# Token forms of the second half in two pieces, with weight forms between them, and another order of the first block's products

## The chip, the cores and the metric

One Trainium2 chip, of which the kernel uses one core. The metric is device microseconds from launch to end of one execution, lower is better. The core has a matrix engine (TensorE, PE in the profile; its weight loads are PEld), VectorE (DVE), ScalarE (ACT), GpSimd (POOL) and SyncE (SP); each works through its own instruction queue in order and waits on semaphores of the others. POOL and SP issue the transfers between the chip's main memory and the on-chip buffers.

## What is computed

Two pre-norm residual layers on 1024 tokens of width 1024, and a final norm, all in float32. The parts that the change touches are the channel MLP of both layers and the input projection of the second layer's gating unit:

```python
for layer in range(DEPTH):                      # DEPTH = 2
    h = rms_norm(x, mix_norm[layer])
    if layer % 2 == 0:
        ...                                     # gated recurrence and attention
    else:
        gated = chunked_gmlp(h @ gm_w_in[o], gm_ln_g[o], gm_ln_b[o], gm_ws[o], gm_bs[o])
        mix = gated @ gm_w_out[o]
    x = x + mix
    h = rms_norm(x, mlp_norm[layer])
    x = x + jnp.square(jax.nn.relu(h @ mlp_w1[layer])) @ mlp_w2[layer]
return rms_norm(x, final_norm)
```

`chunked_gmlp` applies gelu to both halves of its input, a layer norm to the second (`v`), mixes `v` inside chunks of 128 tokens and multiplies.

## The kernel before

**Tokens and halves.** The activations stand with features on partitions, in two token halves of 512: half 0 and half 1, each as four tiles of 128 x 1024 (`xp[half]`, two feature blocks of 512 columns in one tile).

**Split numbers.** Every matmul operand is split into a high part (rounded by ScalarE to the fp32r type) and a low part (VectorE: value minus high part). A product of two split operands takes three matmuls (`mm3`: L181 high x high, L182, L183 with the low parts). A *form* is such a pair of tiles: token forms (`make_form`, L190 and L191) and weight forms (`split2`, L738 and L739; high part `whi` on ScalarE, low part `wlo` on VectorE).

**Seven products.** Big products are done by a seven-product scheme of Strassen's kind on 2 x 2 blocks, named P1 to P7. Each of the seven needs a token form (two tiles, `k2` = 0 and 1: a sum or difference of half 0 and half 1) and a weight form (a sum of weight quarters). P1 and P2 need half 0 only. P7 needs the difference inside half 1, and P6, P5, P4 and P3 are made from it on VectorE one after another, by sums and splits (`half1_forms`).

**Stages.** `inward` computes the MLP's first product in column blocks b = 0, 1, ... of 512 hidden features; (b,p) is product p of block b, 24 matmuls. `gmlp` does the gating unit's `v` projection, with weights moving and tokens stationary; there a product comes in two steps kp = 0, 1, (p,kp), 24 matmuls each. `outward` brings the MLP back to 1024 features and prepares half 0 of the next stage while it ends, so that P1 and P2 can start at once.

**The entries.** Half 1 of a stage's input is complete only as the stage begins. Its norm and token forms are therefore made by a `lead`, a list of three steps that `inward` and `gmlp` run ahead of their first three products: sums of squares, `rms1` (the norm's factor) and `forms1`. `forms1` spreads the factor over a tile (`spread`, L767), scales half 1 with eight VectorE instructions (`scaled`, L772) and makes all of P7, P6, P5, P4 and P3 (`half1_forms`, L845 to L866). This happens at three places: entry I (first layer's MLP, from about 611 us), entry II (`gmlp`, about 1290) and entry III (second layer's MLP, about 2070). The second call of `inward` (the gating unit's `u` half) has no lead.

**What sets the order.** The program text is written in the order in which work is wanted, and the framework then puts each engine's queue in order by its own estimate of when things are ready, so neighbouring products' matmuls can stand interleaved. Ahead of each product the weight forms of the next two are asked for (`LEAD = 2`); ahead of a lead step, those of the product itself and one more. A group's weights come from `a_forms` in the fixed order P1, P2, P7, P6, P4, P5, P3, since each sum builds on the one before (L888, L891, L894, L896). There are three buffers for weight forms (`U_W`), six for raw weights (`U_RAW`), four accumulators of two PSUM banks (`pair_ps`) that also serve the norm. Results of the first products are held back (`held`) until the third product is issued, and then taken out by `after1` (`evict` in `gmlp`): a copy by ScalarE (L944, L1220) or an addition by VectorE (L1006, L1225), a further VectorE step for relu squared (L1007), and a store by POOL (L939).

The order of the first two blocks before is (0,P1), (0,P2), (1,P1), (1,P2), (0,P6), (0,P7), (0,P5), (0,P4), (0,P3), (1,P6), (1,P7), (1,P5), (1,P4), (1,P3).

Of the kernel before, what the change touches and what calls it, by code (L numbers as in the profile page):

```python
# [109 lines left out]
def trunk(tc, x_in, mix_norm, mlp_norm, w1, w2, ab_in, ab_out, lb_logits, hgrn_norm,  # L110
# [4 lines left out]
    with ctx:  # L115
# [575 lines left out]
        P1, P2, P6, P7, P5, P4, P3 = range(7)  # L691
        SEQ = [P1, P2, P6, P7, P5, P4, P3]
# [100 lines left out]
        def make_form(f, k2, src):  # L793
            t = new_form(f, k2)
            split(t.hi, t.lo, src)

        class Entry:
# [31 lines left out]
                self.r = self.rms(1, one_bank)  # L829

            def forms1(self):
                half1_forms(self.gcol, spread(self.r, self.two[1][1], one_bank()))

                spare.extend(self.two[1][::-1])

            def lead(self):
                return [lambda: self.squares(1, (0, 1)), self.rms1, self.forms1]

        spare = []

        def half1_forms(gcol, rb):
            for m2 in range(4):
                spill(1, m2)
            for k2 in range(2):
                for k0 in (0, 2):  # L845
                    for j in range(2):
                        scaled(1, 2 * (k0 + k2) + j, gcol, rb)

            sums = [u_tile("fh") for k2 in range(2)]
            b11, b21, b12, b22 = xp[0][0:2], xp[0][2:4], xp[1][0:2], xp[1][2:4]  # L850
            for k2 in range(2):
                vec.tensor_tensor(out=sums[k2], in0=b22[k2], in1=b12[k2], op=ALU.subtract)
                make_form(P7, k2, sums[k2])
            make_form(P3, 0, b22[0])
            for k2 in range(2):
                vec.scalar_tensor_tensor(out=sums[k2], in0=sums[k2], scalar=-1.0, in1=b11[k2],
                                         op0=ALU.mult, op1=ALU.subtract)
                make_form(P6, k2, sums[k2])
            for k2 in range(2):
                vec.tensor_tensor(out=b12[k2], in0=b11[k2], in1=b12[k2], op=ALU.subtract)  # L860
                make_form(P5, k2, b12[k2])
            for k2 in range(2):
                vec.scalar_tensor_tensor(out=sums[k2], in0=sums[k2], scalar=-1.0, in1=b21[k2],
                                         op0=ALU.mult, op1=ALU.subtract)
                make_form(P4, k2, sums[k2])
            make_form(P3, 1, b22[1])  # L866

        def one_bank():
            return pair_ps()[:, 0, :]
# [33 lines left out]
        def inward(ww, NB, finish, lead, last, extra={}):  # L903
# [66 lines left out]
                                             op0=ALU.mult, op1=ALU.subtract)  # L970
                    store(P4, b, t4)

            order = []
            for b in range(NB):
                todo = [(b, p) for p in SEQ if b != 1 or p not in (P1, P2) or not lead]
                if b == 0 and lead:
                    todo[2:2] = [(1, P1), (1, P2)]
                order += todo
            LEAD = 2
            held = []  # L980
            for i, (b, p) in enumerate(order):
                if i < len(lead):
                    for b2, p2_ in order[i:i + LEAD]:
                        form1(b2, p2_)
                    lead[i]()
                for b2, p2_ in order[i:i + 1 + LEAD]:
                    form1(b2, p2_)
                finish(b, None, None, p, order[i + 1:i + 3], None)
                if i == len(order) - 1:
                    last()  # L990
                held.append((b, p, product1(b, p)))
                if i >= len(lead) - 1:
                    while held:
                        after1(*held.pop(0))
                if p == P6 and b in extra:
                    extra[b]()
# [165 lines left out]
        def gmlp(lead):  # L1162
# [69 lines left out]
            tiles, acc, held = {}, {}, []  # L1232
            for n, (u, p, kp) in enumerate(order):
                if n < len(lead):
                    for o in order[n:n + 2]:
                        form_v(*o)
                    lead[n]()
                for o in order[n:n + 3]:
                    form_v(*o)
                a = form_v(u, p, kp)  # L1240
                fresh = p in (P1, P7, P2)
                if fresh and kp == 0:
                    acc[u, p] = [pair_ps() for _ in range(2)]
                elif kp == 0:
                    acc[u, p] = acc[u, {P6: P1, P5: P6, P3: P5, P4: P7}[p]]
                f = form[p, kp]
                for c in range(2):
                    ps = acc[u, p][c]
                    for s in range(2):
                        tok = slice((2 * c + s) * P, (2 * c + s + 1) * P)  # L1250
                        for k in range(2):
                            mm3(ps[:, s, :], (f.hi[:, k, tok], f.lo[:, k, tok]),
                                (a.hi[:, k, :], a.lo[:, k, :]),
                                fresh and kp == k == 0, kp == k == 1, not fresh)
                if kp == 1:
                    held.append((u, p))
                if n >= len(lead) - 1:
                    while held:
                        evict(*held.pop(0))
            for tb in range(8):  # L1260
# [163 lines left out]
```

## Time and profile before

| | us |
|---|---|
| median of 3 runs | 2743.43 |
| the three runs | 2742.97, 2743.43, 2746.48 |
| the profiled execution | 2744.25 |
| its span, first to last instruction | 2742.3 |
| TensorE busy in the span | 2640.1 |
| VectorE busy | 1820.9 |
| ScalarE busy | 1019.4 |

The profile is one execution on the core. Its timeline view lists instructions of one engine in order of time, with the idle time before them and what ended it in brackets; the view of waits adds these up by who waited for whom; the view of stretches gives each engine's busy time and TensorE's granted clock (1.00 is 2.4 GHz, 0.50 is 1.2 GHz) in chosen stretches. Matmuls overlap: one starts every 0.23 us or so and is shown as 0.39 long.

### The profile page before, as it was taken

How to read it: one execution, taken by the hardware profiler on the slowest of the kernel's cores; microseconds unless marked ns; L12 is line 12 of the kernel's file. 1: busy time of each engine (PE TensorE's matmuls, PEld its weight loads, DVE VectorE, ACT ScalarE, POOL GpSimd, SP SyncE). 2: the span in 40 equal slices, each digit the busy share in tenths (PEclk: the TensorE clock that was granted, in tenths of full speed). 3: DMA queues.
4: the chain of work that ended last, by engine and by line, in shares of the span. 5: the costliest groups of instructions: out<-in, count | busy, mean ns of one | idle time of the engine just before them, and what ended most of it. 6: DMA issues, size and time to landing. Idle time of an engine off the chain costs nothing.

```text
span 2742.3 us, 31530 instructions
## 1 busy us (share of the span) xinstructions
PE 2640.1 (96%) x12489; PEld 2143.1 (78%) x12489; DVE 1820.9 (66%) x2046; ACT 1019.4 (37%) x1281; POOL 152.5 (6%) x261
## 2 busy tenths in 40 slices
PE   8999999997999999999899999999997999999998
PEld 7888867685888878887688887877876888878887
DVE  4545464756766687777855666677778666687774
ACT  4212144543333343343433454443334333343343
POOL 1000000000101100000000100000000111000000
PEclk9999999998999999999999999999998999999999
DMA  4111111332545383444233454565431544483341
GB/s 153 43 32 47 43 35 58 108 108 68 184 140 183 124 301 131 159 162 145 73 119 114 138 194 161 191 255 199 169 131 59 167 151 141 160 305 117 131 159 62
DMA packets 204826, 371.62 MB, mean 136 GB/s; under 512 B 12072, under 2 KB 120328, under 8 KB 204680
## 3 DMA queue, kind: packets, MB, share of 16 engines
q1 hardware_dynamic: 173896, 257.93, 28.5%
q0 software_dynamic: 30784, 111.69, 10.5%
q8 instruction: 98, 1.61, 0.2%
q14 instruction: 48, 0.39, 0.0%
HBM read 253.71 MB, written 115.87 MB: 135 GB/s over the span
## 4 chain that ended last, share of the span: by engine, by line
PE 83%; DVE 9%; issue 3%; DMA 3%; ACT 2%; POOL 0%; SPq 0%; DVEq 0%; ACTq 0%; POOLq 0%
PE acc L182 21%; PE acc L183 21%; PE acc L181 21%; PE mm L181 4%; PE mm L183 4%; PE mm L182 4%; PE sm L393 1%; DVE e L551 1%; PE acc L1354 1%; DVE sig L555 1%; DVE x L772 1%; DMA nx<-v_d 1%; PE po L181 1%; DMA fr<-in_gm_w_out 1%; ACT whi L738 0%
## 5 line engine op out<-in xcount | busy, mean ns | idle before, releaser
L738 ACT ACTIVATE whi<-raw 128x1024 fp32r<-128x1024 f32 x273 | 288.6, 1058 | 956.9 <-PE acc L182 754.0
L739 DVE TENSOR_TENSOR wlo<-raw,whi 128x1024 fp32r<-128x1024 f32 x273 | 333.3, 1221 | 392.8 <-ACT whi L738 389.4
L181 PE MATMUL acc<-f1h,whi 128*128 128x512 f32 x1144 | 454.6, 398 | 11.9 <-ACT f1h L738 8.0
L182 PE MATMUL acc<-f1l,whi 128*128 128x512 f32 x1144 | 454.5, 397 | 2.0 <-DVE f1l L739 1.8
L183 PE MATMUL acc<-f1h,wlo 128*128 128x512 f32 x1144 | 453.7, 397 | 0.4 <-DVE wlo L739 0.4
L181 PEld LDWEIGHTS acc<-f1h,whi 128*128 128x128 f32 x1144 | 214.9, 188 | 67.0 <-ACT f1h L738 10.6
L182 PEld LDWEIGHTS acc<-f1l,whi 128*128 128x128 f32 x1144 | 215.3, 188 | 57.2 <-DVE f1l L739 4.0
L183 PEld LDWEIGHTS acc<-f1h,wlo 128*128 128x128 f32 x1144 | 215.3, 188 | 53.8 <-DVE wlo L739 1.1
L182 PE MATMUL acc<-f1l,fh 128*128 128x512 f32 x616 | 243.7, 396 | 0.0
L181 PE MATMUL acc<-f1h,fh 128*128 128x512 f32 x616 | 243.5, 395 | 0.0
L183 PE MATMUL acc<-f1h,fl 128*128 128x512 f32 x616 | 243.4, 395 | 0.0
L1065 DVE TENSOR_TENSOR x<-x,acc 128x1024 f32<-128x1024 f32 x154 | 187.1, 1215 | 34.9 <-PE acc L183 27.0
L181 PE MATMUL mm<-ah,whi 128*128 128x512 f32 x448 | 181.6, 405 | 0.0
L739 DVE TENSOR_TENSOR f1l<-fb,f1h 128x1024 fp32r<-128x1024 f32 x154 | 181.2, 1217 | 0.2 <-ACT f1h L738 0.2
L183 PE MATMUL mm<-ah,wlo 128*128 128x512 f32 x448 | 179.5, 401 | 0.0
L182 PE MATMUL mm<-al,whi 128*128 128x512 f32 x448 | 178.7, 399 | 0.0
L738 ACT ACTIVATE f1h<-fb 128x1024 fp32r<-128x1024 f32 x154 | 152.0, 1044 | 12.2 <-DMA fb<-f_d 12.2
L181 PEld LDWEIGHTS acc<-f1h,fh 128*128 128x128 f32 x616 | 116.0, 188 | 28.5
L182 PEld LDWEIGHTS acc<-f1l,fh 128*128 128x128 f32 x616 | 115.7, 188 | 28.5
L183 PEld LDWEIGHTS acc<-f1h,fl 128*128 128x128 f32 x616 | 115.7, 188 | 28.2
L939 POOL DMA_DIRECT2D f_d<-x x150 | 80.1, 534 | 751.6 <-DVE x L1007 351.9
L65 DVE TENSOR_TENSOR wlo<-raw,whi 128x1024 fp32r<-128x1024 f32 x44 | 53.8, 1222 | 100.8 <-ACT whi L64 80.7
(281 smaller groups left out, 4903.3 us busy)
## 6 DMA issues: line engine op xcount, KB each, us to landing
fb<-f_d SPq DMA_DIRECT2D x154, 512.0 KB, 4.8
f_d<-x POOLq DMA_DIRECT2D x150, 512.0 KB, 3.3
raw<-in_mlp_w SPq DMA_DIRECT2D x96, 512.0 KB, 4.6
raw<-in_gm_w_in SPq DMA_DIRECT2D x54, 512.0 KB, 4.6
fr<-in_mlp_w SPq DMA_DIRECT2D x32, 512.0 KB, 10.1
raw<-in_ab_w_in SPq DMA_DIRECT2D x28, 512.0 KB, 4.4
x_d<-x POOLq DMA_DIRECT2D x24, 512.0 KB, 2.9
x<-x_d SPq DMA_DIRECT2D x24, 512.0 KB, 7.4
```

The source lines that it names most:

```text
L65: nc.vector.tensor_tensor(out=lo, in0=raw, in1=hi.bitcast(F32), op=ALU.subtract)
L181: pe.matmul(out=ps, lhsT=a[0], rhs=b[0], start=start, stop=False, skip_group_check=s)
L182: pe.matmul(out=ps, lhsT=a[0], rhs=b[1], start=False, stop=False, skip_group_check=s)
L183: last_mm[0] = pe.matmul(out=ps, lhsT=a[1], rhs=b[0], start=False, stop=stop, skip_group_check=s)
L393: mm = pe.matmul(out=p3[:, c, :].rearrange("p (b m) -> p b m", m=m), lhsT=kr[:, c * P:(c + 1) * P], rhs=qv[:, c, :, 1, :], start=True, sto ...
L551: vec.tensor_tensor_scan(out=e[:, 0:w][:, ::-1], data0=keep[:, 0:w][:, ::-1], data1=d1[:, ::-1], initial=init, op0=ALU.mult, op1=ALU.max)
L555: vec.tensor_tensor(out=sig[:, 0:w], in0=sig[:, 0:w], in1=e[:, 1:w + 1], op=ALU.mult)
L738: in_turn("hi", lambda: act.activation(t.hi, raw, AF.Copy))
L739: vec.tensor_tensor(out=t.lo, in0=raw, in1=t.hi.bitcast(F32), op=ALU.subtract)
L772: vec.scalar_tensor_tensor(out=xt[half][k], in0=xt[half][k], scalar=gn[:, gcol + k:gcol + k + 1], in1=rb, op0=ALU.mult, op1=ALU.mult)
L939: nc.gpsimd.dma_start(out=f_d[f][b], in_=flat(t))
L1065: last_add[0] = vec.tensor_tensor(out=t, in0=t, in1=ps, op=op)
```

## The change

`half1_forms` becomes a generator that stops once, after the P7 forms; the rest (P3's first form, P6, P5, P4, P3's second) becomes a fourth lead step, `forms2`. The weight forms asked for ahead of the third and fourth lead step reach one product further (`(i > 1)`, and the same in `gmlp`). With a lead, the first two blocks of `inward` take another order: (1,P2) moves behind (0,P6), P7 comes before P6, and both stand right behind (1,P1). Results are still held until the third product. In `gmlp` the order of products stays.

```diff
@@ -829,12 +829,16 @@
                 self.r = self.rms(1, one_bank)
 
             def forms1(self):
-                half1_forms(self.gcol, spread(self.r, self.two[1][1], one_bank()))
+                self.rest = half1_forms(self.gcol, spread(self.r, self.two[1][1], one_bank()))
+                next(self.rest)
 
                 spare.extend(self.two[1][::-1])
 
+            def forms2(self):
+                assert next(self.rest, None) is None
+
             def lead(self):
-                return [lambda: self.squares(1, (0, 1)), self.rms1, self.forms1]
+                return [lambda: self.squares(1, (0, 1)), self.rms1, self.forms1, self.forms2]
 
         spare = []
 
@@ -851,6 +855,7 @@
             for k2 in range(2):
                 vec.tensor_tensor(out=sums[k2], in0=b22[k2], in1=b12[k2], op=ALU.subtract)
                 make_form(P7, k2, sums[k2])
+            yield True
             make_form(P3, 0, b22[0])
             for k2 in range(2):
                 vec.scalar_tensor_tensor(out=sums[k2], in0=sums[k2], scalar=-1.0, in1=b11[k2],
@@ -970,17 +975,15 @@
                                              op0=ALU.mult, op1=ALU.subtract)
                     store(P4, b, t4)
 
-            order = []
-            for b in range(NB):
-                todo = [(b, p) for p in SEQ if b != 1 or p not in (P1, P2) or not lead]
-                if b == 0 and lead:
-                    todo[2:2] = [(1, P1), (1, P2)]
-                order += todo
+            order = [(b, p) for b in range(NB) for p in SEQ]
+            if lead:
+                order[:14] = [(0, P1), (0, P2), (1, P1), (0, P7), (0, P6), (1, P2), (0, P5), (0, P4),
+                              (0, P3)] + [(1, p) for p in SEQ[2:]]
             LEAD = 2
             held = []
             for i, (b, p) in enumerate(order):
                 if i < len(lead):
-                    for b2, p2_ in order[i:i + LEAD]:
+                    for b2, p2_ in order[i:i + LEAD + (i > 1)]:
                         form1(b2, p2_)
                     lead[i]()
                 for b2, p2_ in order[i:i + 1 + LEAD]:
@@ -989,7 +992,7 @@
                 if i == len(order) - 1:
                     last()
                 held.append((b, p, product1(b, p)))
-                if i >= len(lead) - 1:
+                if i >= len(lead) - 2:
                     while held:
                         after1(*held.pop(0))
                 if p == P6 and b in extra:
@@ -1232,7 +1235,7 @@
             tiles, acc, held = {}, {}, []
             for n, (u, p, kp) in enumerate(order):
                 if n < len(lead):
-                    for o in order[n:n + 2]:
+                    for o in order[n:n + 2 + (n > 1)]:
                         form_v(*o)
                     lead[n]()
                 for o in order[n:n + 3]:
@@ -1254,7 +1257,7 @@
                                 fresh and kp == k == 0, kp == k == 1, not fresh)
                 if kp == 1:
                     held.append((u, p))
-                if n >= len(lead) - 1:
+                if n >= len(lead) - 2:
                     while held:
                         evict(*held.pop(0))
             for tb in range(8):
```

What this does to the queues, first at entry I. VectorE there, from the first sum of half 1's forms (`fh_5694`, the P7 sum) on, before and after; `f1l` is the low part of P7's token forms, `fl` of P3's first, `nx_5592<-nx_5592,acc` the addition of (0,P2)'s result, `wlo_5743` the low part of (1,P2)'s weight:

```order
L852 TENSOR_TENSOR fh_5694<-x_4963,x_4961 128x1024
L852 TENSOR_TENSOR fh_5695<-x_4964,x_4962 128x1024
L191 TENSOR_TENSOR fl_5707<-x_4963,fh_5706 128x1024
L191 TENSOR_TENSOR f1l_5698<-fh_5694,f1h_5697 128x1024
L191 TENSOR_TENSOR f1l_5703<-fh_5695,f1h_5702 128x1024
L856 SCALAR_TENSOR_TENSOR fh_5694<-fh_5694,x_4104 128x1024
L856 SCALAR_TENSOR_TENSOR fh_5695<-fh_5695,x_4105 128x1024
```

```order
L856 TENSOR_TENSOR fh_5694<-x_4963,x_4961 128x1024
L856 TENSOR_TENSOR fh_5695<-x_4964,x_4962 128x1024
L1009 TENSOR_TENSOR nx_5592<-nx_5592,acc_5648 128x1024
L191 TENSOR_TENSOR f1l_5698<-fh_5694,f1h_5697 128x1024
L191 TENSOR_TENSOR f1l_5703<-fh_5695,f1h_5702 128x1024
L1010 SCALAR_TENSOR_TENSOR nx_5592<-nx_5592 128x1024
L739 TENSOR_TENSOR wlo_5743<-raw_5736,whi_5742 128x1024
L191 TENSOR_TENSOR fl_5747<-x_4963,fh_5746 128x1024
L861 SCALAR_TENSOR_TENSOR fh_5694<-fh_5694,x_4104 128x1024
```

The addition of (0,P2), its next step and (1,P2)'s weight form now stand among the first forms, and P3's first form behind P7's. ScalarE at the same place, before and after; `f1h` is P7's token form, `whi_5742` the weight form of (1,P2), `nx_5591<-acc` and `nx_5592<-acc` are evictions of (1,P1) and (0,P1):

```order
L738 ACTIVATE whi_5745<-raw_5575 128x1024
L767 ACTIVATE nx_5592<-acc_5678 128x512
L944 ACTIVATE nx_5591<-acc_5754 128x1024
L944 ACTIVATE nx_5592<-acc_5606 128x1024
L190 ACTIVATE fh_5706<-x_4963 128x1024
L190 ACTIVATE f1h_5697<-fh_5694 128x1024
L190 ACTIVATE f1h_5702<-fh_5695 128x1024
```

```order
L738 ACTIVATE whi_5674<-raw_5575 128x1024
L767 ACTIVATE nx_5592<-acc_5678 128x512
L738 ACTIVATE whi_5742<-raw_5736 128x1024
L949 ACTIVATE nx_5591<-acc_5706 128x1024
L949 ACTIVATE nx_5592<-acc_5606 128x1024
L190 ACTIVATE f1h_5697<-fh_5694 128x1024
L190 ACTIVATE f1h_5702<-fh_5695 128x1024
```

The weight form of (1,P2), which stood further up, now stands between L767 and the evictions.

The end of the forms on VectorE, entry I, before and after; `fr_5732` and `fr_5772` are the low part of P4's first form, `fl_5737` and `fl_5777` of its second, `wlo_5751` of (0,P6)'s weight, `wlo_5817` of (0,P5)'s:

```order
L191 TENSOR_TENSOR fr_5732<-fh_5694,fr_5731 128x1024
L891 TENSOR_TENSOR raw_5575<-raw_5575,raw_5585 128x1024
L1006 TENSOR_TENSOR nx_5592<-nx_5592,acc_5653 128x1024
L191 TENSOR_TENSOR fl_5737<-fh_5695,fh_5736 128x1024
L739 TENSOR_TENSOR wlo_5751<-raw_5575,whi_5750 128x1024
L1007 SCALAR_TENSOR_TENSOR nx_5592<-nx_5592 128x1024
```

```order
L191 TENSOR_TENSOR fr_5772<-fh_5694,fr_5771 128x1024
L899 TENSOR_TENSOR raw_5585<-raw_5585,raw_5583 128x1024
L1009 TENSOR_TENSOR nx_5591<-nx_5591,acc_5846 128x1024
L191 TENSOR_TENSOR fl_5777<-fh_5695,fh_5776 128x1024
L739 TENSOR_TENSOR wlo_5817<-raw_5585,whi_5816 128x1024
L1010 SCALAR_TENSOR_TENSOR nx_5591<-nx_5591 128x1024
L191 TENSOR_TENSOR fl_5781<-x_4964,fh_5780 128x1024
L901 TENSOR_TENSOR raw_5575<-raw_5575,raw_5581 128x1024
```

Before, (0,P6)'s weight sum (L891) and its low part stand here; now P5's do, and P6's have moved ahead of the scaling of half 1.

Entry II on VectorE, before and after, behind the sums for P7 (`fh_9898`, `fh_9907`); `wlo_9986` and `wlo_9948` are the low part of the weight of (P7,1):

```order
L852 TENSOR_TENSOR fh_9898<-x_7852,x_7850 128x1024
L191 TENSOR_TENSOR fl_9910<-x_7851,fh_9909 128x1024
L191 TENSOR_TENSOR f1l_9901<-fh_9897,f1h_9900 128x1024
L191 TENSOR_TENSOR f1l_9906<-fh_9898,f1h_9905 128x1024
L856 SCALAR_TENSOR_TENSOR fh_9897<-fh_9897,x_7693 128x1024
L856 SCALAR_TENSOR_TENSOR fh_9898<-fh_9898,x_7694 128x1024
```

```order
L856 TENSOR_TENSOR fh_9907<-x_7852,x_7850 128x1024
L739 TENSOR_TENSOR wlo_9948<-raw_9809,whi_9947 128x1024
L191 TENSOR_TENSOR f1l_9910<-fh_9906,f1h_9909 128x1024
L191 TENSOR_TENSOR f1l_9915<-fh_9907,f1h_9914 128x1024
L191 TENSOR_TENSOR fl_9952<-x_7851,fh_9951 128x1024
L861 SCALAR_TENSOR_TENSOR fh_9906<-fh_9906,x_7693 128x1024
```

And at the end of the forms, where `raw_9807<-raw_9807,raw_10023` is the sum for the weight of (P6,0):

```order
L191 TENSOR_TENSOR fr_9935<-fh_9897,fr_9934 128x1024
L739 TENSOR_TENSOR wlo_9986<-raw_9809,whi_9985 128x1024
L1225 TENSOR_TENSOR nx_9733<-nx_9733,acc_9956 128x1024
L191 TENSOR_TENSOR fl_9940<-fh_9898,fh_9939 128x1024
L1225 TENSOR_TENSOR nx_9732<-nx_9732,acc_9957 128x1024
L1183 TENSOR_TENSOR raw_9807<-raw_9807,raw_10023 128x1024
L1209 BN_STATS bn_9787<-nx_9733 128x6
```

```order
L191 TENSOR_TENSOR fr_9977<-fh_9906,fr_9976 128x1024
L1228 TENSOR_TENSOR nx_9733<-nx_9733,acc_9918 128x1024
L191 TENSOR_TENSOR fl_9982<-fh_9907,fh_9981 128x1024
L1228 TENSOR_TENSOR nx_9732<-nx_9732,acc_9919 128x1024
L1186 TENSOR_TENSOR raw_9807<-raw_9807,raw_10023 128x1024
L1212 BN_STATS bn_9787<-nx_9733 128x6
```

One row, the weight's low part, has moved from the second list's place to the first's; the rows from L1225 (now L1228) on have as many ahead of them as before.

## Rows read from the trace of the kernel before

**Rows 1.** The page, part 1: busy time, share, instructions of each engine.
```profile
PE 2640.1 (96%) x12489; PEld 2143.1 (78%) x12489; DVE 1820.9 (66%) x2046; ACT 1019.4 (37%) x1281; POOL 152.5 (6%) x261
```

**Rows 2.** Waits of TensorE: us in total, times, longest.
```profile
PE acc L181 <- ACT whi L738: 35.6, 3, 15.9
...
PE acc L182 <- DVE wlo L739: 9.9, 2, 9.0
```

**Rows 3.** Timeline of TensorE, entry I: start, us, line, tiles, idle before.
```profile
657.33 0.39 PE L182 MATMUL acc<-f1l,whi 128*128 128x512 f32 x1
657.56 0.40 PE L183 MATMUL acc<-f1h,wlo 128*128 128x512 f32 x1
...
679.41 0.80 PE L181 MATMUL acc<-fb,whi 128*128 128x512 f32 x1 [15.86 <-ACT whi L738]
...
692.94 0.39 PE L181 MATMUL acc<-fr,whi 128*128 128x512 f32 x1
...
709.28 0.39 PE L181 MATMUL acc<-fb,whi 128*128 128x512 f32 x1
```

**Rows 4.** Timeline of TensorE, entry III.
```profile
2109.82 0.79 PE L181 MATMUL acc<-fb,whi 128*128 128x512 f32 x1 [15.80 <-ACT whi L738]
...
2139.57 0.39 PE L181 MATMUL acc<-fb,whi 128*128 128x512 f32 x1
```

**Rows 5.** Timeline of TensorE, entry II.
```profile
1324.79 0.62 PE L181 MATMUL acc<-whi,f1h 128*128 128x512 f32 x2
1334.39 0.80 PE L182 MATMUL acc<-wlo,f1h 128*128 128x512 f32 x1 [8.97 <-DVE wlo L739]
...
1343.56 0.50 PE L182 MATMUL acc<-wlo,fb 128*128 128x512 f32 x1 [0.97 <-DVE wlo L739]
```

**Rows 6.** Timeline of VectorE, entry I.
```profile
653.58 5.38 DVE L772 SCALAR_TENSOR_TENSOR x<-x,gn,nx 128x512 f32<-128x512 f32 x8
658.88 2.36 DVE L852 TENSOR_TENSOR fh<-x 128x1024 f32<-128x1024 f32 x2
...
677.05 1.22 DVE L891 TENSOR_TENSOR raw<-raw 128x1024 f32<-128x1024 f32 x1
...
688.40 1.22 DVE L896 TENSOR_TENSOR raw<-raw 128x1024 f32<-128x1024 f32 x1
...
693.85 1.22 DVE L888 TENSOR_TENSOR raw<-raw 128x1024 f32<-128x1024 f32 x1 [2.38 <-DMA raw<-in_mlp_w]
```

**Rows 7.** Stretches: length, busy PE PEld DVE ACT POOL, granted clock, DMA share, GB/s.
```profile
510.00:516.00 6.00, 3.51 (x20) 2.79 (x19) 3.08 (x5) 4.00 (x10) 0.00 (x0) 1.00 0.47 166
...
679.40:684.00 4.60, 4.59 (x10) 3.34 (x11) 4.60 (x6) 1.96 (x2) 0.58 (x1) 0.50 0.01 4
...
993.40:998.20 4.80, 1.26 (x4) 0.48 (x3) 4.80 (x6) 4.73 (x6) 0.00 (x0) 1.00 0.05 20
998.30:1001.60 3.30, 3.30 (x8) 2.62 (x9) 3.30 (x4) 2.19 (x3) 0.00 (x0) 0.50 0.56 181
...
1334.40:1339.60 5.20, 5.20 (x12) 4.12 (x13) 5.20 (x6) 4.98 (x5) 1.25 (x2) 0.50 0.25 99
```

**Rows 8.** Timeline of ScalarE, entry I.
```profile
657.99 2.10 ACT L944 ACTIVATE nx<-acc 128x1024 f32<-128x1024 f32 x2 [5.00 <-PE acc L183]
...
660.93 2.00 ACT L190 ACTIVATE f1h<-fh 128x1024 fp32r<-128x1024 f32 x2
```

**Rows 9.** Timeline of VectorE, entry III.
```profile
2089.30 2.35 DVE L852 TENSOR_TENSOR fh<-x 128x1024 f32<-128x1024 f32 x2
```

**Rows 10.** Timeline of VectorE, entry II.
```profile
1317.22 1.22 DVE L191 TENSOR_TENSOR fl<-x,fh 128x1024 fp32r<-128x1024 f32 x1
...
1333.12 1.22 DVE L739 TENSOR_TENSOR wlo<-raw,whi 128x1024 fp32r<-128x1024 f32 x1
...
1342.31 1.20 DVE L739 TENSOR_TENSOR wlo<-raw,whi 128x1024 fp32r<-128x1024 f32 x1
```

**Rows 11.** The page, part 6: DMA issues, KB each, us to landing.
```profile
fr<-in_mlp_w SPq DMA_DIRECT2D x32, 512.0 KB, 10.1
```

## The prediction

> **What bounds the kernel now.** Read the page's engine lines first: TensorE is busy 96% of the span [rows 1], so time comes off only where it stands. The view of waits then names who holds it: three waits of a product's first matmul for a weight form's high part, 35.6 us in all, the longest 15.9, and two for a low part, the longest 9.0 [rows 2]. The TensorE timeline puts them at the three entries: 15.86 us at 679.41 in entry I [rows 3], 15.80 at 2109.82 in entry III [rows 4], 8.97 and 0.97 in entry II [rows 5].
>
> The VectorE timeline says why. In entry I it scales the second half from 653.58 and from 658.88 puts out one 1024-column instruction every 1.135 us without a pause until 688.40 (26 steps in 29.52 us) [rows 6]. TensorE has work for four products and is through it at 679.41 - 15.86 = 663.55 [rows 3]; the fifth product, (0,P6), wants a weight form whose sum (L891) stands at 677.05, behind all the token forms [rows 6]. So each entry is bound by the order of VectorE's queue, not by its amount alone.
>
> The clock is the second cost. After the gap the granted clock is 0.50, the lower level of 1.2 GHz, from 679.4 to 684.0, with 10 matmuls started [rows 7]. At the upper level a matmul starts every 0.227 us (72 from 692.94 to 709.28 [rows 3]), so 4.6 us would hold 20.3: the gap costs another 10.3 x 0.227 = 2.3 us.
>
> **Entries I and III, step by step.** Nothing is added or removed; matmuls, forms and loads are the same and stand otherwise. From (1,P6) on, TensorE's order is again that of before, so entry I's gain is how much earlier that product starts than 709.28 [rows 3].
>
> 1. ScalarE's queue. The weight form of (1,P2) now stands ahead of two evictions and the P7 token forms (second pair of lists). Its buffer comes free when (1,P1) has read it, 657.33 + 0.39 = 657.7 [rows 3]. Queued behind: two evictions (a pair takes 2.10 us) and the two P7 token forms (2.00) [rows 8]. At about 1.03 us each the first token form is done at 657.7 + 4 x 1.03 = 661.8. TensorE ends (1,P1) at 657.56 + 0.40 = 657.96 and waits for it: this added wait costs 3.8 us.
>
> 2. VectorE's queue (first pair of lists). Two sums from 658.88, then the addition of (0,P2)'s result, which also frees the accumulator that (1,P2) wants, then the P7 low part: three steps on, 658.88 + 3 x 1.135 + 1.22 = 663.5 [rows 6]. TensorE gets three matmuls in before that, then runs: the rest of P7, then (1,P2) and (0,P6) interleaved as their forms come. These 69 matmuls, 15.7 us, last to about 680 and fill what was the gap.
>
> 3. The next limit is the end of the same VectorE chain (third pair of lists). The low part of P4's second form is 22 steps after the first sum: 658.88 + 22 x 1.135 + 1.22 = 685.1. TensorE arrives at 680.5 and spends the time to there in three short waits (first P4 low part at 681.7, weight form of P5 at 683.9, this one at 685.1) with ten matmuls between them.
>
> 4. From 685.1 there are 63 matmuls to (1,P6): the rest of P4 and P5, and P3. Their weights are in time: P5's low part, one step on, at 686.2 against 685.1 + 6 x 0.227 = 686.5; P3's, five further, at 691.9 against 694.0; (1,P6)'s, six further, at 698.7 against 699.4. 63 x 0.227 = 14.3, so (1,P6) starts at 699.4 instead of 709.28: **9.9 us**.
>
> Cross-check: the gap and its clock cost 15.86 + 2.3 = 18.2. Instead come 3.8, then 1.0 (to 663.5, less three matmuls), 2.3 in the short waits (4.6 less ten matmuls) and about 1 us of low clock: 8.1, a difference of 10.1.
>
> The clock after the broken start has a row: from 993.4 to 998.2 TensorE was busy 1.26 us of 4.8, and the next 3.3 us were granted 0.50 [rows 7]; the start here is as thin. That costs up to 6.5 x 0.227 = 1.5 us, but falls before 680, where TensorE waits for VectorE anyway: hidden, at most 1 us if that cover is gone.
>
> Entry III has the same order. The first sum is at 2089.30 [rows 9]: 2089.30 + 22 x 1.135 + 1.22 + 14.3 = 2129.8 against 2139.57 [rows 4]: **9.8 us**.
>
> SyncE keeps its order; the loads of block 1's last two quarters are freed at VectorE's subtraction for P5, at about 682.8 (20 steps on) instead of 688.5, and are used from 689.5 (27 steps on). POOL's stores keep their order.
>
> **Entry II.** Here only one instruction moves in front of the wait: the low part of the second P7 weight, from 1333.12 [rows 10] to third behind the sums, about 1317.2 (fourth pair of lists). So (P7,1) runs at once, 1324.79 to 1330.4 (24 x 0.227), and the 8.97 us go. But the next product, (P6,0), wants the low part that stands at 1342.31 in VectorE's queue [rows 10], and that place is the same: as many instructions are ahead of it. It starts its third matmul at 1343.56 either way [rows 5]. The gain is nought, and something is lost: before, the low clock after the gap (0.50 from 1334.4 to 1339.6 [rows 7]) was over when that product began; now TensorE comes to it from some 13 us with two matmuls in them. I take the price from the nearest row, that after 15.86 us: 4.6 us at the lower level, **2.3 us lost**. The ends are 3.3 us at it (8 matmuls where 14.5 fit: 1.5) and 5.2 us (12 where 22.9 fit: 2.5) [rows 7]; a loss of nothing is kept as the outer end, since the two matmuls may start the recovery early.
>
> **Sum.** 9.9 + 9.8 - 2.3 = 17.4 us. On the profiled execution, 2744.25 (span 2742.3 and 1.95 around it): 2726.9. That execution is 0.8 above the median of three, 2743.43, so the forecast is **2726** us, -0.63%. Bounds of each entry I and III: 9.9 if VectorE never pauses, about 7 if an eviction on ScalarE delays a token form by one instruction (1.1) and a further low clock costs 1.5.
>
> **Rivals.**
> A. The clock falls a second time, in the three short waits. For: 1.26 of 4.8 us busy was followed by the lower level [rows 7]. Against: from 510 to 516 TensorE was busy 3.51 of 6 us and was granted 1.00 throughout [rows 7]; ten matmuls in 680.5 to 685.1 are some 2.5 of 4.6, much nearer to that. Price: 3.3 us at the lower level after 685.1, no longer hidden, 1.5 us in each entry: 2729. The Trainium skill speaks for it (TensorE: Matmul & The Clock Gate, "A second HAM failure mode: psum-queue depth-cycling": short idles between groups of matmuls, if frequent, make the clock swing between its levels and cost a re-warming between bursts). By that rule the sum would be 14.4 and not 17.4; the row at 510 does not bear it out at this density.
> B. VectorE's chain is the wall in all three entries as in II. Then the wait only moves, nothing is gained in I and III, and II loses its 2.3: 2743.4 + 2.3 = 2746, within 0.2%. For: VectorE passes the same amount by 688. Against: in I and III TensorE has three products (P7, (1,P2), P6) to do under that chain, by the places above; in II one.
> C. The whole gap goes: 15.86 + 15.80 + 2 x 2.3 and entry II's 2.3 lost give 2743.4 - 36.3 + 2.3 = 2709. Against: places 2 and 3, at which VectorE's queue is late by the same rate.
> D. Slower, by the loads. VectorE's sum for block 1's P7 weight, at about 689.5, waits for a load freed at 682.8, and all later weights are queued behind it. Before, it was released one step ahead of the row at 688.40, so at 688.5, and VectorE stood 2.38 us for it until 693.85: 5.4 us [rows 6]: it would land at 688.2. VectorE has 1.3 us of room and TensorE 2.1 more. A load of 10.1 us, the median of the slowest kind [rows 11], costs TensorE 1.3. To turn the whole change slower it must eat half of 17.4 in each entry: 8.7 + 3.4 + 5.4 = 17.5 us after its release; it then gives 2744 to 2750.
>
> **How the numbers follow.** Forecast 0.70, A 0.16, B 0.06, C 0.04, D 0.04. The range goes from the gain with nothing lost in entry II (19.7, so 2723.7, and 1 us of scatter) to A with the weaker bounds of I and III and the loss of 2.5 (2743.4 - 2 x 7 + 2.5 = 2731.9) and the 3 us by which one run shown stands above the median: **2722.5 to 2735**; B, C and D stay outside, 0.14. About 0.2%, 5.5 us, is what a measurement of this kernel can tell from no change. Faster by more: forecast, A and C, 0.90; within: B, 0.06; slower: D, 0.04.
>
> **What the changed profile would show.** Right: the largest TensorE wait of entries I and III is about 3.8 us and names the P7 token form; VectorE shows no pause between the first sum and the low part of P4's second form; (1,P6) starts some 40.5 us after the first sum of the second half (50.4 and 50.3 before [rows 3, 4, 6, 9]); in entry II a wait of 9 to 13 us stands before (P6,0), and the granted clock is 0.50 behind it. Wrong: granted clock 0.50 behind 685 (A), an unbroken long wait at P7 or P6 (B), a wait of VectorE for a load near the sum for block 1 (D).

## The result and the profile after

The changed kernel takes **2728.53 us** (median of four runs, 2726.83 to 2731.06) against 2744.95 for the kernel before (four runs); the ratio is 0.994 with a 95% interval from 0.9922 to 0.9957. The forecast was 2726 us, the profiled execution was forecast at 2726.9 and took 2726.83 (span 2724.7). The forecast was counted from 2743.43, the median of the three runs then known; a fourth run has since put that median at 2744.95, and the medians are now 16.4 us apart.

TensorE's busy time hardly moved, from 2640.1 us to 2644.2; what went is standing time. The page's engine lines and the view of waits (who waited for whom: us in total, times, longest), to be read as [rows 1] and [rows 2]:

```profile
PE 2644.2 (97%) x12489; PEld 2145.3 (79%) x12489; DVE 1820.9 (67%) x2046; ACT 1019.7 (37%) x1281; POOL 152.6 (6%) x261
...
PE acc L181 <- ACT whi L738: 15.3, 4, 10.2
...
PE acc L181 <- ACT f1h L190: 7.4, 2, 3.7
...
PE acc L182 <- DVE wlo L739: 1.7, 1, 1.7
```

The two waits of 15.8 us are gone. The longest wait for a weight form is now 10.2 us, in entry II, and a new kind stands here: two waits of 3.7 us for a token form's high part.

TensorE in entry I, after (start, us, engine, line, operation; in brackets the wait before and who ended it), to be held against [rows 3], and two rows of entry III, the last against [rows 4]:

```profile
661.74 1.53 PE L181 MATMUL acc<-f1h,whi 128*128 128x512 f32 x2 [3.73 <-ACT f1h L190]
...
682.04 0.50 PE L182 MATMUL acc<-fr,whi 128*128 128x512 f32 x1 [0.30 <-DVE fr L191]
...
684.27 0.50 PE L181 MATMUL acc<-fr,whi 128*128 128x512 f32 x1 [0.58 <-ACT whi L738]
...
685.45 0.50 PE L182 MATMUL acc<-fl,whi 128*128 128x512 f32 x1 [0.44 <-DVE fl L191]
...
699.90 0.39 PE L181 MATMUL acc<-fb,whi 128*128 128x512 f32 x1
...
2085.29 1.53 PE L181 MATMUL acc<-f1h,whi 128*128 128x512 f32 x2 [3.68 <-ACT f1h L190]
...
2123.32 0.39 PE L181 MATMUL acc<-fb,whi 128*128 128x512 f32 x1
```

Read the first row as the wait that the change adds, the next three as the three short waits of the forecast, and 699.90 as the start of (1,P6), 9.38 us before the 709.28 of [rows 3]. VectorE, after, against [rows 6], with the first sum of entry III in the last row, against [rows 9]:

```profile
658.94 2.35 DVE L856 TENSOR_TENSOR fh<-x 128x1024 f32<-128x1024 f32 x2
...
662.34 2.36 DVE L191 TENSOR_TENSOR f1l<-fh,f1h 128x1024 fp32r<-128x1024 f32 x2
...
673.95 1.23 DVE L191 TENSOR_TENSOR fb<-fh,fb 128x1024 fp32r<-128x1024 f32 x1 [0.17 <-ACT fb L190]
...
684.17 1.23 DVE L191 TENSOR_TENSOR fl<-fh 128x1024 fp32r<-128x1024 f32 x1
...
689.84 1.22 DVE L893 TENSOR_TENSOR raw<-raw 128x1024 f32<-128x1024 f32 x1
...
2082.49 2.36 DVE L856 TENSOR_TENSOR fh<-x 128x1024 f32<-128x1024 f32 x2
```

From the first sum to the low part of P4's second form (684.17) it pauses once, for 0.17 us. The sum for block 1 (689.84) waits for no load. Entry II, TensorE and then VectorE, against [rows 5] and [rows 10]:

```profile
1331.09 1.22 PE L181 MATMUL acc<-whi,fb 128*128 128x512 f32 x2 [10.24 <-ACT whi L738]
1334.05 0.79 PE L182 MATMUL acc<-wlo,fb 128*128 128x512 f32 x1 [1.73 <-DVE wlo L739]
...
1347.26 0.39 PE L181 MATMUL acc<-whi,fr 128*128 128x512 f32 x1
```

```profile
1305.35 2.35 DVE L856 TENSOR_TENSOR fh<-x 128x1024 f32<-128x1024 f32 x2
...
1332.79 1.21 DVE L739 TENSOR_TENSOR wlo<-raw,whi 128x1024 fp32r<-128x1024 f32 x1
```

The same two marks in entry II before the change, the first sum and the first matmul on P4's forms (`fr`):

```profile
1314.95 2.35 DVE L852 TENSOR_TENSOR fh<-x 128x1024 f32<-128x1024 f32 x2
...
1354.12 0.39 PE L181 MATMUL acc<-whi,fr 128*128 128x512 f32 x1
```

The wait only moved, from before (P7,1) to before (P6,0). The low part that ends it stands 1332.79 - 1305.35 = 27.4 us behind the first sum; before it was 1342.31 - 1314.95 = 27.4 as well. The clock, in the view of stretches (start:end, length, busy PE PEld DVE ACT POOL, granted clock, DMA share, GB/s), against [rows 7]:

```profile
661.70:665.00 3.30, 3.26 (x6) 1.96 (x7) 3.30 (x4) 1.88 (x2) 0.00 (x0) 0.50 0.01 2
...
681.50:685.50 4.00, 2.68 (x11) 1.40 (x9) 4.00 (x5) 2.35 (x4) 0.00 (x0) 1.00 0.23 62
685.50:690.00 4.50, 4.50 (x20) 3.69 (x21) 4.50 (x5) 0.99 (x1) 0.53 (x1) 1.00 0.64 203
...
1334.00:1339.30 5.30, 5.25 (x12) 4.13 (x13) 4.14 (x4) 2.01 (x2) 0.00 (x0) 0.50 0.02 3
```

It is at the lower level behind the 3.7 us wait and behind the wait of entry II, and at the upper level behind the three short waits.

**Where the time went.** (1,P6) starts 40.96 us after the second half's first sum in entry I and 40.83 in entry III (50.40 and 50.27 before), so 9.4 us gained in each. In entry II the first matmul on P4's forms starts 41.9 us after the first sum, 39.2 before: 2.7 lost. That makes 16.1. The other 1.3 of the 17.4 us between the two profiled executions lie outside the entries. From (1,P6) of entry III to the final norm's matmuls it is 1.1 us less, and that mostly at one wait for a token form, 1.22 us before and 0.30 after:

```profile
2422.55 0.74 PE L181 MATMUL acc<-f1h,whi 128*128 128x512 f32 x2 [1.22 <-ACT f1h L738]
```

```profile
2405.17 0.73 PE L181 MATMUL acc<-f1h,whi 128*128 128x512 f32 x2 [0.30 <-ACT f1h L738]
```

### The profile page after: what moved, and what is told of

Same layout as the page of the kernel before. It is cut to its first block, busy times and chain, and to the rows that moved or that the text cites. A ratio compares the mean times of both kernels' runs of the same rounds, so it can differ in the third digit from the quotient of the medians.

```text
span 2724.7 us, 31525 instructions
## 1 busy us (share of the span) xinstructions
PE 2644.2 (97%) x12489; PEld 2145.3 (79%) x12489; DVE 1820.9 (67%) x2046; ACT 1019.7 (37%) x1281; POOL 152.6 (6%) x261
## 4 chain that ended last, share of the span: by engine, by line
PE 83%; DVE 8%; issue 3%; DMA 3%; ACT 2%; POOL 0%; SPq 0%; DVEq 0%; ACTq 0%; POOLq 0%
PE acc L182 21%; PE acc L181 21%; PE acc L183 21%; PE mm L181 4%; PE mm L183 4%; PE mm L182 4%; PE sm L393 1%; DVE e L551 1%; PE acc L1357 1%; DVE sig L555 1%; DMA x<-x_d 1%; DMA nx<-v_d 1%; ACT whi L738 1%; PE po L181 1%; DMA fr<-in_gm_w_out 1%
```

## Experiments

Two places are used as marks in each kernel, both counted, in us, from the second half's first sum: (1,P6) in entries I and III, and the first matmul on P4's forms in entry II. The last column is the median of the kernel before, timed beside the run.

| kernel | I | II | III | time, us | before beside it |
|---|---|---|---|---|---|
| before | 50.4 | 39.2 | 50.3 | 2744.95 | |
| changed | 41.0 | 41.9 | 40.8 | 2728.53 | 2744.95 |
| MLP entries alone | 41.2 | 39.2 | 40.7 | 2728.48 | 2745.24 |
| gmlp alone | 49.6 | 42.0 | 50.2 | 2746.55 | 2745.24 |
| order alone | 45.8 | 39.2 | 46.4 | 2738.45 | 2745.24 |
| split alone | 46.0 | 39.2 | 44.5 | 2733.30 | 2745.24 |
| two more VectorE steps | 44.6 | 44.0 | 46.7 | 2739.71 | 2745.87 |
| P5's sums on GpSimd | 41.6 | 43.3 | 41.6 | 2729.29 | 2745.87 |
| P6 weights ahead in gmlp | 40.7 | 30.6 | 40.7 | 2716.00 | 2745.87 |

### The MLP entries alone, gmlp alone

```diff
+            def forms12(self):
+                self.forms1()
+                self.forms2()
...
+            def lead3(self):
+                return [lambda: self.squares(1, (0, 1)), self.rms1, self.forms12]
...
-            gmlp(e.lead())
+            gmlp(e.lead3())
...
-                    for o in order[n:n + 2 + (n > 1)]:
+                    for o in order[n:n + 2]:
...
-                if n >= len(lead) - 2:
+                if n >= len(lead) - 1:
```

> The change in the two MLP entries (I and III) alone; gmlp (entry II) keeps the three-step lead and makes all token forms in one piece, as before. Theory (VectorE's chain sets entries I and III, entry II loses by the clock): (1,P6) starts 41 us after the second half's first sum in I and III, as in the changed kernel (40.96 there); entry II is that of before, a wait of about 9 us ahead of (P7,1), low clock spent on that product, none on (P6,0). The time is that of the changed kernel less entry II's loss, which its trace gives as 9.60 - 6.86 = 2.7 us: before - 19, about 2725.8 against 2728.5. Rival (the low clock of entry II costs nothing in the end, since something later in gmlp is late anyway): the same time as the changed kernel, 2728.5.

The other kernel undoes the change in `inward` instead, in the same way, and its order too.

> The change in gmlp (entry II) alone; inward keeps the order of before and all token forms in one piece. Theory: entries I and III are those of before (gaps of 15.8 us); in II a wait of about 10 us stands ahead of (P6,0) in place of 9 ahead of (P7,1), the low clock falls on (P6,0): before + 2.7, about 2747.6, so slower by 0.1%. Rival (the loss is made up later): before + 0.

Stage by stage both theories hold to 0.3 us, but for 49.6 in place of 50.4 in one entry: entries I and III belong to the one half of the change, entry II to the other. In the whole time it is not so plain. The first kernel took 2728.48, ratio 0.9942 (0.9927 to 0.9956), which is what its rival said; the second 2746.55, ratio 1.0002 (0.9993 to 1.0011), an interval that holds both the 2.7 us of its theory and nothing. So the first was run again beside the changed kernel, with more executions.

> The changed kernel again, timed beside the next run on the same chip. Theory and rival alike: 2728 to 2729, as before.

> The change in the two MLP entries alone, again, with more executions: it and the changed kernel came out at the same time, though entry II takes 2.7 us less from the first sum to the first matmul on P4's forms (39.2 against 41.9). Theory (entry II's loss is real and the two profiled executions differ elsewhere by scatter of the same size): 2.7 us below the changed kernel timed beside it, and in its profile the rest outside entry II agrees with the changed kernel's to about 1 us. Rival (the loss is taken back elsewhere every time): the same time within 1 us, and the profile again shows 3 to 4 us more than the changed kernel's outside entry II.

Now it is 2727.97 (2725.45 to 2728.55) for the changed kernel and 2725.88 (2724.02 to 2730.09) without its part in `gmlp`: 2.1 us apart, the side that the theory wants, with ranges that overlap. Entry II again takes 39.2 us against 42.1. The profiled executions, though, are 2727.29 and 2727.38, so that the second is again some 3 us longer outside entry II, as the rival said. Part of this stands ahead of everything in which the two kernels differ: the first sum of entry I is at 658.9 and 658.8 in the two profiles of the changed kernel and at 659.9 and 660.7 in the two of the other. The rest lies at other places in the one pair of profiles than in the other. That the stage loses 2.7 us is shown; whether the whole time loses it is not, since it is no larger than such differences.

### The order alone, the split alone

Both leave `gmlp` as it was before, as in the kernel with the MLP entries alone. The order alone gives `inward` the lead of three steps, `lead3`, too:

```diff
-            lead = [lambda: e.squares(1, range(4))] + e.lead()[1:]
+            lead = [lambda: e.squares(1, range(4))] + e.lead3()[1:]
...
-            inward(w1[1], HID // 512, relu2, e.lead(), first)
+            inward(w1[1], HID // 512, relu2, e.lead3(), first)
...
-                    for b2, p2_ in order[i:i + LEAD + (i > 1)]:
+                    for b2, p2_ in order[i:i + LEAD]:
...
-                if i >= len(lead) - 2:
+                if i >= len(lead) - 1:
```

> The new order of products in inward with all token forms in one piece (no split anywhere, gmlp as before). In its queues the weight form of (0,P6) already stands ahead of the token forms, since its sum is asked for as the third product; only the low part of the weight of (1,P2) stays behind 18 VectorE steps. Theory (VectorE's queue): that low part is out at 658.9 + 19 x 1.135 + 1.2 = 681.7, then 92 matmuls x 0.227 = 20.9 to (1,P6): 43.7 us after the first sum against 41.0 of the changed kernel and 50.4 of before. So before - 13.4, about 2731.5: the order carries two thirds of the gain, the split one third. Rival 1 (the split is what brings the P6 weight forward, without it the wait stays): before + 0, 50.4 us. Rival 2 (the order alone does all): before - 19, 2726.

The other one keeps the split, and the order of before:

```diff
-            order = [(b, p) for b in range(NB) for p in SEQ]
-            if lead:
-                order[:14] = [(0, P1), (0, P2), (1, P1), (0, P7), (0, P6), (1, P2), (0, P5), (0, P4),
-                              (0, P3)] + [(1, p) for p in SEQ[2:]]
+            order = []
+            for b in range(NB):
+                todo = [(b, p) for p in SEQ if b != 1 or p not in (P1, P2) or not lead]
+                if b == 0 and lead:
+                    todo[2:2] = [(1, P1), (1, P2)]
+                order += todo
```

> The split with the old order of products in inward ((1,P2) ahead of the P6 product), gmlp as before. In its queues the low part of the (0,P6) weight stands among the scalings and waits for a buffer that (1,P1) frees at 657.7, so the first sum starts about 1.8 us later than in the changed kernel; then the same chain: low part of the second P4 form 21 steps on, at 685.8, and 74 matmuls (nine of them of (1,P7), which the changed kernel does later) to (1,P6). TensorE has (1,P2) to do until 663.5, so no wait for the P7 token form of 3.7 us. Theory: the end is set by VectorE's chain all the same, so taking the 3.7 us wait away gains nothing: before - 17.5 with 1.5 us either way, about 2727.5. Rival (the 3.7 us wait is a real cost of the new order): 7 us faster than the kernel with the change in the MLP entries alone, about 2719.

Each gained, and both gained less than expected: 6.8 us where 13.4 was said, ratio 0.9976 (0.9967 to 0.9986), for the order, and 11.9 where 17.5 was said, ratio 0.9959 (0.9945 to 0.9974), for the split. Neither half alone brings the gain, so all the rivals fall, and the sizes of the theories too. The view of stretches shows what they had left out. Entry I of the order alone:

```profile
680.70:685.40 4.70, 0.88 (x4) 0.34 (x3) 4.26 (x5) 2.13 (x3) 0.58 (x1) 0.93 0.00 0
685.40:688.00 2.60, 2.60 (x6) 2.11 (x7) 2.60 (x3) 0.00 (x0) 0.00 (x0) 0.50 0.48 202
```

Entry I of the split alone:

```profile
681.40:687.10 5.70, 1.06 (x4) 0.39 (x3) 4.37 (x5) 3.02 (x3) 0.53 (x1) 0.87 0.00 0
687.10:690.00 2.90, 2.90 (x7) 2.32 (x8) 2.90 (x3) 1.72 (x2) 0.00 (x0) 0.50 0.44 181
```

TensorE gets four matmuls into some 5 us, where the changed kernel gets eleven into 4.0, and the granted clock falls to 0.50 behind them, where no later wait for VectorE covers it. This is rival A, in other kernels. With the order alone, the low part of the weight of (1,P2) ends its wait at 685.36, 23.4 us after the first sum (22.8 expected), and the 92 matmuls from there to (1,P6) take 22.4 us instead of 20.9; in entry III 23.5. With the split alone, 79 matmuls from 687.09 take 20.6 us, where 79 x 0.227 = 17.9.

The split alone also takes away most of the 3.7 us wait (1.2 and 0.6 us stand there instead). Without the 2.7 us of clock, and without the nine matmuls of (1,P7) that it does early (2.0 us), its (1,P6) would be at 46.0 - 2.7 - 2.0 = 41.3 in entry I, and by the same sum at 39.9 in entry III (2.6 us of clock), against the changed kernel's 41.0 and 40.8. So the wait of 3.7 us looks free, or nearly so, as long as VectorE's chain ends last; this is worked out, not run by itself.

The mark leaves out one more cost of the split alone. VectorE does a weight's sum and a low part among the eight scalings of half 1 there, which it does ahead of them in the changed kernel:

```profile
654.12 0.74 DVE L772 SCALAR_TENSOR_TENSOR x<-x,gn,nx 128x512 f32<-128x512 f32 x1
654.79 1.22 DVE L903 TENSOR_TENSOR raw<-raw 128x1024 f32<-128x1024 f32 x1
...
659.90 1.22 DVE L739 TENSOR_TENSOR wlo<-raw,whi 128x1024 fp32r<-128x1024 f32 x1
...
661.70 2.35 DVE L863 TENSOR_TENSOR fh<-x 128x1024 f32<-128x1024 f32 x2
```

So the first sum itself comes 661.70 - 654.12 = 7.6 us after the scaling begins, in entry III as well, against 5.3 in [rows 6]: 2.3 us in each entry that the expectation had at 1.8.

### Two VectorE steps more, two less

```diff
                 make_form(P4, k2, sums[k2])
+                if k2 == 0:
+                    for _ in range(2):
+                        vec.tensor_tensor(out=form[P4, 0].lo, in0=sums[0], in1=form[P4, 0].hi.bitcast(F32),
+                                          op=ALU.subtract)
```

> The changed kernel with two more VectorE instructions at each entry: the low part of the first P4 form is computed three times. Theory (VectorE's chain sets the end of each entry): each costs its 1.135 us, so (1,P6) starts 2.3 us later, 43.2 us after the first sum, and the low part of (P6,0) in entry II comes 2.3 us later: 6.8 us in all, 2735.3. Rival (TensorE's own waits for ScalarE and its work set it): (1,P6) stays at 41 us, 2728.5.

(1,P6) moved by 3.6 and 5.9 us, entry II by 2.1, and the time is 2739.71, 11 us above the changed kernel where 6.8 was expected. The rival falls. The surplus is the clock once more: in entry III TensorE starts three matmuls in 4.9 us and then runs at the lower level for 5.4.

```profile
2112.20:2117.10 4.90, 0.82 (x3) 0.30 (x2) 4.90 (x6) 1.06 (x1) 0.00 (x0) 0.87 0.37 107
2117.10:2122.50 5.40, 5.39 (x13) 4.22 (x14) 5.40 (x5) 2.92 (x3) 0.53 (x1) 0.50 0.53 182
```

The 69 matmuls from 2117.11 to (1,P6) take 18.3 us instead of 69 x 0.227 = 15.7. Taken off, 46.7 - 2.7 = 44.0 is left, and by the same sum 43.1 in entry I (1.5 us), against 43.2 expected. The edit also changed TensorE's queue a little: TensorE does some twenty other matmuls ahead of those on P4's second form there, and its last wait is for the repeated step itself.

The opposite was tried by moving the two sums for P5 to GpSimd.

```diff
-                vec.tensor_tensor(out=b12[k2], in0=b11[k2], in1=b12[k2], op=ALU.subtract)
+                pool_e.tensor_tensor(out=b12[k2], in0=b11[k2], in1=b12[k2], op=ALU.subtract)
```

> The changed kernel with the two sums of the P5 token forms on GpSimd instead of VectorE, at all three entries. That takes two steps out of VectorE's chain ahead of the low part of the second P4 form. Theory (that chain sets (1,P6)): (1,P6) 2 x 1.135 = 2.3 us earlier in entries I and III, so 38.7 us after the first sum; in II the low part of the (P6,0) weight comes 2.3 us earlier too: 6.8 us in all, 2721.7. Rival 1 (ScalarE's splits of these sums stand ahead of the P6 splits and wait for a slow GpSimd): (1,P6) later than 41 us, the kernel slower than 2728.5. Rival 2 (VectorE is slowed while GpSimd runs): VectorE's steps show more than 1.135 us there.

Both rivals came true, in different entries, and nothing is gained: 2729.29. VectorE and GpSimd of this kernel in entry I:

```profile
661.57 1.21 DVE L1009 TENSOR_TENSOR nx<-nx,acc 128x1024 f32<-128x1024 f32 x1
662.70 5.58 DVE L191 TENSOR_TENSOR f1l<-fh,f1h 128x1024 fp32r<-128x1024 f32 x2
...
660.74 6.45 POOL L865 TENSOR_TENSOR x<-x 128x1024 f32<-128x1024 f32 x2 [13.22 <-DVE fh L856]
```

and GpSimd, ScalarE and, in the second list, VectorE of the same kernel in entry II:

```profile
1307.53 12.46 POOL L865 TENSOR_TENSOR x<-x 128x1024 f32<-128x1024 f32 x2 [13.22 <-DVE fh L856]
...
1317.64 1.06 ACT L190 ACTIVATE fr<-x 128x1024 fp32r<-128x1024 f32 x1 [7.43 <-POOL x L865]
```

```profile
1312.99 2.35 DVE L861 SCALAR_TENSOR_TENSOR fh<-fh,x 128x1024 f32<-128x1024 f32 x2
1318.74 2.33 DVE L191 TENSOR_TENSOR fr<-x,fr 128x1024 fp32r<-128x1024 f32 x1 [3.40 <-ACT fr L190]
```

In entry I two VectorE steps take 5.58 us instead of 2.36, which eats the 2.3 us that two steps fewer would give. In entry II it is GpSimd that takes 12.46 us, where it took 6.45 in entry I, and ScalarE, whose split of that sum stands ahead of the P6 splits, waits 7.43 us for it.

### A second break, in gmlp

Entry II loses because the weight form of (P6,0) still stands behind all token forms. The cure follows from that: break the forms once more, after P6, and ask for P6's weights there. `lead_v` has five steps: `forms2` makes P3's first form and P6's, a new `forms3` the rest.

```diff
                 make_form(P6, k2, sums[k2])
+            yield True
...
-            gmlp(e.lead())
+            gmlp(e.lead_v())
...
-                    for o in order[n:n + 2 + (n > 1)]:
+                    for o in order[n:n + 2 + (n > 1) + (n > 3)]:
...
-                if n >= len(lead) - 2:
+                if n >= 2 or not lead:
```

The last line keeps results held until the third product, as in the changed kernel. `inward` still makes the rest in one piece.

> The changed kernel, and in gmlp a second break of the token forms: after the P6 forms, with both weight forms of P6 asked for ahead of the rest (P5, P4, P3). inward is that of the changed kernel. Theory for entry II (what is lost there is that the (P6,0) weight form stands behind all token forms): t is the second half's first sum; VectorE puts out the (P6,0) weight's sum at t + 14.8 to 16.0, ScalarE its high part at t + 17.0, VectorE the low part at t + 18.4, and TensorE is through with P7 at t + 15.5. So waits of about 1.5 and 0.9 us in place of 10.2 and 1.7, no low clock, and the next product, (P4,0), starts at about t + 29.5 instead of t + 41.9 (before: t + 39.2). That is 12.4 us off the changed kernel's 2728.5: 2716. Rival (the loads of the weights or the evictions are late next in gmlp): the wait moves to P4 or P5 and little is gained, 2724 to 2729.

It takes **2716.00 us** (2712.63 to 2719.40), ratio 0.9888 (0.9872 to 0.9905) against the kernel before, and beats both kernels. TensorE in entry II, and VectorE's first sum:

```profile
1324.53 0.73 PE L181 MATMUL acc<-whi,fb 128*128 128x512 f32 x2 [1.66 <-ACT whi L738]
1325.79 0.55 PE L182 MATMUL acc<-wlo,fb 128*128 128x512 f32 x1 [0.53 <-DVE wlo L739]
...
1337.94 0.62 PE L181 MATMUL acc<-whi,fr 128*128 128x512 f32 x2
```

```profile
1307.37 2.35 DVE L866 TENSOR_TENSOR fh<-x 128x1024 f32<-128x1024 f32 x2
```

Waits of 1.66 and 0.53 us stand where 10.24 and 1.73 stood, and the P4 forms are reached at 1337.94 - 1307.37 = 30.6 us (29.5 expected). The missing 1.1 us is the clock, which I had expected to hold. It costs even a little more: the 46 matmuls from 1325.79 to 1337.94 take 12.15 us, where 46 x 0.227 = 10.4.

```profile
1322.80:1325.90 3.10, 0.91 (x4) 0.41 (x4) 3.10 (x5) 1.06 (x1) 0.41 (x1) 1.00 0.49 192
1325.90:1328.00 2.10, 2.10 (x6) 1.67 (x7) 2.10 (x3) 1.10 (x2) 0.00 (x0) 0.55 0.04 8
```

## Why the prediction was right

**Entries I and III, steps 1 to 4.** Each step can be found in the rows. The wait for the P7 token form is 3.73 and 3.68 us (3.8 said). The P7 low part starts at 662.34, so it is out 1.22 us later, at 663.56 (663.5 said). The short waits end at 682.04, 684.27 and 685.45 (681.7, 683.9 and 685.1 said). (1,P6) starts at 699.90 (699.4 said), and in entry III 40.8 us after the first sum (40.5). The gain is 9.4 in each instead of 9.9 and 9.8. Of the 0.4 us by which (1,P6) is later after the first sum than said, 0.3 came in on VectorE, where the low part of P4's second form starts at 684.17 (683.9 by the count), 0.17 of it by the pause. One term of step 3 was mis-sized and hidden, as the forecast said such a term would be: the low clock behind the added wait lasted from 661.7 to 667.2, 5.5 us and not the 3.3 of the row that was taken, and TensorE came to P4 at 681.36 and not at 680.5. The three short waits are so much shorter, 0.30 + 0.58 + 0.44 = 1.3 us in place of 2.3. The run with two steps more shows that VectorE's chain sets the end of the entry and does not only stand beside it.

**The clock behind the short waits (rival A).** It stayed at 1.00, as the row at 510 to 516 [rows 7] had made likelier: 2.68 us busy in 4.0. But the rival is nearer than its chance of 0.16 suggests. Three of the kernels, with waits at the same place and three or four matmuls between them instead of eleven, show it in each MLP entry, at 1.5 to 2.7 us a time. What the new order adds to the split can be read from the same rows: (1,P2) and P6 interleaved keep TensorE late enough for VectorE, so that the remaining waits are short and have matmuls between them, where the split alone paid 2.7 and 2.6 us of clock; and the two steps among the scalings, 2.3 us in each entry, stand ahead of them. The section of the Trainium skill cited at that rival (TensorE: Matmul & The Clock Gate, "A second HAM failure mode: psum-queue depth-cycling") says that frequent short idles between groups of matmuls make the clock swing. Its case is one of cycling through accumulator banks, while TensorE waits for operands here; the falling clock itself is what those three kernels show behind their short waits, and the changed one does not.

**Entry II.** The step was right in place and sign: the wait moved to (P6,0), 10.24 + 1.22 + 1.73 = 13.2 us from (P7,1)'s end with two matmuls in them (some 13 said), the low part no earlier than before, the clock at 0.50 behind it. The term that was mis-sized is its price: I took 2.3 us from the row behind the gap of 15.86, and it is 2.7, a little beyond the end of 2.5 that I kept. The low clock lasted 5.3 us, like the 5.2 of the row behind 8.97, the same entry's own, and not the 4.6 that I took; the product's third matmul is 0.1 us later by itself. It was 5.3 us again in the changed kernel's second profile and with gmlp alone, behind the same waits, but 3.8 us with P5's sums on GpSimd, behind waits of 11.21 and 3.04 us in the same place. So the length of the wait did not give it, and no run shows what does. The runs of parts alone show the 2.7 us in the stage, while their whole times show it no better than the scatter allows.

**The sum.** 9.4 + 9.4 - 2.7 = 16.1 where 17.4 was said. That the profiled execution came out at 2726.83 against 2726.9 is therefore luck by 1.3 us, which came from outside the entries. The medians do not have it: they are 16.4 us apart, close to the 16.1 of the entries, and 2728.53 stands 2.5 us above the forecast, 1.5 of it because the kernel before now stands that much above the median that the forecast was counted from.

**Rivals B, C and D.** B (the wait only moves) holds in entry II alone, as said. C falls by size: 9.4 us are gained in an entry, not the 15.86 + 2.3 of its gap and clock. D falls: VectorE's sum for block 1 stands at 689.84 without a wait for its load.

## What to carry to other kernels

When an engine stands because one small instruction is queued behind a long series on another, count that engine's queue in steps from a fixed instruction: the place of the last operand that is wanted, times the time of a step, gave the gain of entries I and III to half a microsecond here, and the same count told where a wait would only move (entry II) and where a second break would cure it. In the runs of a half alone it gave the waits and missed the clock behind them. A wait that is left in front of such a chain may cost nothing; several short waits with few matmuls between them cost their own length here and 1.5 to 2.7 us of clock after it. And GpSimd, idle as it stood, was not a free place for VectorE's elementwise work.

## What the runs showed of the hardware

GpSimd and VectorE slowed each other. In entry I two VectorE steps took 5.58 us instead of 2.36 beside GpSimd's two sums. In entry II the first GpSimd sum took 10.09 us and the second 2.42 (the longest and the shortest of the six in the kernel); the first ended at 1317.62, 2.3 us after VectorE's unbroken series did (1312.99 + 2.35 = 1315.34), and VectorE's step at 1318.74, beside the second, took 2.33 us instead of 1.21. VectorE's step at 661.57, which has one input from an accumulator, took its usual 1.21 us beside GpSimd's sums, while the two behind it, with both inputs in the on-chip buffer, did not. The Trainium skill says the same (SBUF — State Buffer, "Who interferes with whom"): a VectorE instruction with two inputs there contends with a GpSimd instruction that reads it, one with at most one such input does not (some fast modes aside), and the one that issues first keeps the other out. The rows agree on the inputs; in which order the two were issued was not tried apart.

What a broken stretch cost on the clock went with what lay between the waits. In the rows above, eleven matmuls in 4.0 us (2.68 busy) were followed by 1.00, three or four in 3.1 to 5.7 us (0.82 to 1.06 busy) by 0.50 or 0.55.
